# Rests and waits of a hand-written schedule: a two-layer trunk, GLA and sparse attention, on one core

## The chip, the cores and the metric

One core of a Trainium2 chip runs the whole computation as one program. TensorE (PE) does the matrix products, VectorE (DVE) and ScalarE (ACT) the elementwise work, GpSimd (POOL) a little, and SyncE (SP) issues nearly all DMA transfers. The metric is the device time of one execution in microseconds (us), as the median of several.

## What is computed

The reference, cut to the two layers that run (x is 1024 tokens by 1024 features, float32):

```python
def reference(x, p, positions, ...):
    for i in range(DEPTH):                       # DEPTH = 2: gla_mixer, then dsa_mixer
        y = mixer_i(x)
        x = layer_norm(ALPHA * x + y, ln_g[i], ln_b[i])
        x = x + (p[i] @ ple_w[i]) * sigmoid(x @ ple_gate_w[i])
    return x

def gla_mixer(x, ...):       # 4 heads, chunks of 64, dk 256, dv 512
    q, k, v, z, a = split(x @ w_in)
    g = log_sigmoid(a @ w_a2 + b_a) / 16; G = cumsum(g) in the chunk
    o = tril((q e^G)(k e^-G)^T) v + (q e^G) S    # S = e^G_last S + (k e^(G_last-G))^T v
    return (norm(o) * gn_g * silu(z)) @ w_out

def dsa_mixer(x, ...):       # 16 heads of 128, one k and one v for all of them
    q, k, v, z, qi, ki, wi = split(x @ w_in); rope on q, k, qi, ki
    score = sum over 8 index heads of relu(qi ki^T) * wi, causal
    keep the 256 keys of highest score for each query
    return (softmax(q k^T, on the kept keys) v * silu(z)) @ w_out
```

## The kernel before

Every product is made of three: operands are split into a high part and a remainder (`split`, L419 on ACT makes the high part, L411 on DVE subtracts), and high x high, low x high and high x low are summed. Weights are split on the way in as well: `wst` is loaded, ACT makes `whi` (L189) and DVE `wlo` (L191, L193).

The tokens go through in two halves of 512 (HT). Layer 0 (GLA) runs half 0 and half 1, four heads each (GH = 4). Inside a head, chunk pairs c = 0 to 3 pass four steps, s1 to s4; s3 makes the output `ot` from PE's `o` (the DVE copy L785), s4 transposes it on PE (`oT`), multiplies by z (L849) and splits the product into `u` (L411), which the output projection reads as `pb<-whi,u`. For some c the way goes by DRAM in squares (`od`, L801, L807) and ends in L826 and L823 instead; in the last head c = 3 goes by `oT` in both halves, c = 2 only in half 0. Then come the layer norm, the gate (L1002, L1000, L1001), and the new x, stored as `x2s` (L1464) and split for layer 1. Layer 1 (sparse attention) has, for each half, slots -1 to 15, one for each head: products of q, scores S with the selection as an added bias, softmax, transposes of the weights through DRAM (`sqd`, `PT`), split of those (`ph` on ACT, L1679; `PT` on DVE, L1677), the product with v (`o`), and the output projection with its sum in y (L878). A slot of half 0 is some 11 to 22 us long.

What sets the order is a planner that runs while the program is written. `Flow` keeps a planned PE time, `fl.now`, which each matmul advances; steps are put into a heap with due times (`fl.at`, `after`, `chain`) and are written into the program when the planned time has reached theirs. `fl.ripe(t)` holds a step back to planned time t, in tries 0.3 apart; `fl.need(have)` runs due steps until something is there. Engines then take their instructions strictly as written, so the plan decides who stands behind whom, and semaphores decide when each may go.

Two kinds of work are spread thinly over others by a `Background`, one step each `gap` of planned time, none before `due`:

```python
def pace(self, now):
    if self.gen is not None and now >= self.due:
        self.due = max(self.due, now - 2.0) + self.gap
        self.step()
```

`bg3` splits layer 1's weights ahead during layer 0 (`split_ahead`, gap 2.06): for each of 130 cuts of 128x512, a load into `pst` (L223), the high part `phi` on ACT (L233), its store `whs` (L235), the remainder on DVE (L237), its store `wls` (L239). What is left of it at the end of layer 0 is written out at once (`bg3.finish()`, L1517). `bg` runs the rope tables first and, in half 0 of layer 1, the selection (`topk_steps`): for each of the bits of a threshold one count on DVE (L1197, tile 640 wide) and three on ACT (L1241, tiles 768 to 1024 wide) with a few small DVE rows (L1247, L1248, L1250); for the last bit the three tiles are read again from DRAM (`sc<-sc_s`, L1234) and all four are counted on DVE, then L1202 and the rows after it make the bias of each tile (to L1270). `bg.finish()` (L1940) writes out what is left when half 0 ends.

`load_p` (L899) loads two tiles of the token embeddings p for the gate and splits them after a wait; `q_phase` (L1551) puts q of a head through its rope (L1052 to L1057) and splits it a wait of 3.0 later.

Of the kernel before, what the change touches and what calls it, by code (L numbers as in the profile page):

```python
# [23 lines left out]
HT = 512  # L24
NK = 8
GH = 4
# [251 lines left out]
def trunk_kernel(ctx, tc, x_tok, x_T, p_T, pos, freq, g_q, g_k, g_v, g_z, g_a, g_a2, g_ba, g_gn, g_o,  # L278
# [134 lines left out]
    def split(hi, lo, src, done=None):  # L413

        def second():
            lo_part(lo, src, hi)
            if done:
                done()
        chain((0, lambda: act.activation(hi, src, AF.Copy)), (0.9, second))  # L419
# [253 lines left out]
    def core_steps(u):  # L673
# [92 lines left out]
        def s3(c):  # L766
            def f():
                cs = slice(c * 128, c * 128 + 128)
                fl.req(("A", c) in st, v[c] is not None, not has_state(c) or ("S", c) in st)
                fl.ripe(st["At", c] + 2.2)  # L770
                Ah, Al = st.pop(("A", c))
                vh, vl = v[c]
                ps = pp.tile([128, 512], F32, tag="o", name="o")
                ops = [(Ah, vh), (Al, vh), (Ah, vl)]
                if has_state(c):
                    for d, (sh, sl) in enumerate(st.pop(("S", c))):
                        ops += [(qh[:, d, cs], sh), (ql[:, d, cs], sh), (qh[:, d, cs], sl)]
                for i, (l, r) in enumerate(ops):
                    mm(ps, l, r, i == 0, i == len(ops) - 1)
                ot = lp.tile([128, 512], F32, tag="ot", name="ot", bufs=2)  # L780
                if by_square(c):
                    dve.transpose(ot.rearrange("p (m b i) -> p b m i", m=4, b=4), ps)  # L782
                    after(2.2, lambda: squares_out(c, ot))
                else:
                    dve.tensor_copy(ot, ps)  # L785
                junk = lp.tile([128, 512], BF16, tag="junk", name="junk")
                act.activation(junk, ps, AF.Square, accum_out=u["ss"][:, c:c + 1])  # L787
                st["o", c] = ot
                st["ot", c] = fl.now
                u["late"] = c == 3  # L790
                if c < 3:
                    after(0.3, lambda: make_S(c + 1))
            return f
# [41 lines left out]
        def s4(c):  # L835
            def f():
                if by_square(c):
                    return
                cs = slice(c * 128, c * 128 + 128)
                fl.req(("o", c) in st, "z" in u, h == 0 or u["prev"].get("out", 0) > c)  # L840
                fl.ripe(st["ot", c] + (2.6 if h == GH - 1 else 1.1))
                ot = st.pop(("o", c))
                ps = pp.tile([128, 4, 128], F32, tag="oT", name="oT")
                for b in range(4):
                    fl.transpose(ps[:, b], ot[:, b * 128:b * 128 + 128], ident)
                uf = lp.tile([128, 4, 128], F32, tag="uf", name="uf", bufs=2)
                uh, ul = t2k("u", F32R), t2k("u", F32R)

                chain((0, lambda: dve.tensor_mul(uf, ps, u["z"][:, :, cs])),  # L849
                      (0.8, lambda: split(uh, ul, uf.rearrange("p b t -> p (b t)"), lambda: made(c, uh, ul))))  # L850
            return f
# [43 lines left out]
    def load_p(layer, half, alloc, wait, stage):  # L895
        P = []
        for k in range(2):
            st = stage(k)
            nc.sync.dma_start(st, p_T[layer, k, :, half * HT:half * HT + HT])  # L899
            ph, pl = alloc(), alloc()  # L900
            after(wait, lambda ph=ph, pl=pl, st=st: split(ph, pl, st))
            P.append((ph, pl))
        return P
# [142 lines left out]
    def rope(x, c, s, swap, tmp, then, wait=1.2):  # L1046
        ab = []

        def first():
            ab[:] = tmp()[:x.shape[0]], tmp()[:x.shape[0]]  # L1050
            a, b = ab
            dve.tensor_mul(b, x, c)  # L1052
            dve.stream_shuffle(a, x, swap)  # L1053
            dve.tensor_mul(a, a, s)

        def second():
            dve.tensor_add(x, *ab)  # L1057
        chain((0, lambda: None), (0.8, first), (1.6, second), (wait, then))
# [484 lines left out]
    def q_phase(st, h, X):  # L1543
        def ev(ps):
            qf = small_tile("qf")
            fl.need(lambda: h < 2 or st.get(("A", h - 2)) == 3)
            qh, ql = small_tile("q", F32R, 4), small_tile("q", F32R, 4)

            def done():
                st["q", h] = qh, ql  # L1550
            act.activation(qf, ps, AF.Copy)  # L1551
            rope(qf[0:32], tabs[0], tabs[1], swap_h, tmp2, lambda: split(qh, ql, qf, done), 3.0)

        yield from fm_block(("dq", h), X, ev)

# [294 lines left out]
    for half in range(NH):  # L1850
# [12 lines left out]
        S = [attend(st, h, half, ap, sq) for h in range(16)]  # L1863
        for h, units in enumerate(plan, -1):
            start = st["slot"] = fl.now
            bg.gap = 1.4 if h == 15 else 1.75 if h > 3 and h % 4 < 2 else 1.5
            if h == 15:
                fl.at(start + 5.0, lambda: setattr(bg, "due", max(bg.due, fl.now + 24.0)))
            dur = sum(len(u[1]) if u[0] == "o" else 1 for u in units) * B + core * (1.0 if h >= 0 else 0.5)
            if h >= 0:  # L1870
                _, parts, pvs, _, loads, scale = S[h]
                lead = 9.0 if half else 7.4
                step = (dur - lead - 2.4) / len(parts)
                if half:
                    fl.at(start + 1.5, loads[1])
                    early, first, gap = 3, 6.6, 1.2
                else:
                    early, first, gap = 3, max(5.0, 21.5 - last_dur), 1.3
                fl.at(start + (5.0 if half else 3.5), scale[1])
                for i in range(early):  # L1880
                    fl.at(start + first + gap * i, parts[i])
                spread(parts[early:], start + lead + early * step, dur - lead - 2.4 - early * step)
                if h == 15 and half:
                    spread(pvs, start + 10.2, 4.2)
                else:
                    spread(pvs, start + lead + 2.9, dur - lead - 2.4)
            if h < 15:
                first, _, _, stores, loads, scale = S[h + 1]
                spread(first, start + 0.3, 5.8 if half else 4.4)
                for i, f in enumerate(stores):  # L1890
                    fl.at(start + (10.0 if half else 7.0) + 0.5 * i, f)
                fl.at(start + (dur - 3.0 if h == 14 or h < (1 if half else 5) else 12.0 if half else 8.5), scale[0])
                if half:
                    fl.at(start + (max(dur - 1.0, 18.0) if h >= 0 else 16.0), loads[0])
                else:
                    fl.at(start + 13.0, loads[0])
            last_dur = dur
            if h == 14:
                Pt = load_p(1, half, lambda: small_tile("q", F32R, 4), dur + 2.5,
                            lambda k: xp.tile([128, HT], F32, tag="xst", name="xst", bufs=2))  # L1900
            if h == -1:
                if half:
                    yt = new_y()
                y5 = yt.rearrange("p k (a t i) -> p (k a) t i", a=4, t=4)

                def y(t, a, n, y5=y5):
                    return y5[:, a // 32:(a + n) // 32, t]
                normed = {}

                def to_rows(t, y=y, normed=normed):  # L1910
                    normed[t] = [xp.tile([128, HT], F32, tag="x", name="yn", bufs=16) for _ in range(2)]
                    return [(r.rearrange("p (x i) -> p x i", i=32), y(t, 512 * i, 512)) for i, r in enumerate(normed[t])]

                def rows(t, a, n, normed=normed):
                    return normed[t][a // 512][:, a % 512:a % 512 + n]
                for k in range(NK):
                    fl.at(start + (4.0 if half else 14.0) + 3.0 * k, lambda k=k: back(st, yt, k, kept[half, k]))
            if half == 0 and 4 <= h < 12:
                rows_ahead(1, h - 4, lambda n: xp.tile([128, HT], F32, tag="xst", name="xk", bufs=2), start + 2.0)
            fl.run(*(unit(u) for u in units))  # L1920
        norm, y_done = norm_steps(y, l1, EPS / ALPHA ** 2, to_rows, (0, 1))
        if half == 0:
            X = XT()
            feed_by(feed_x2(X, 1), fl.now + 21.0, 2.3)
        for u in last_outs:
            fl.run(unit(u, norm if u[1:2] == ((7,),) else None))
        fl.drain()
# [77 lines left out]
```

## Time and profile before

| | us |
|---|---|
| median of 3 runs | 1933.72 (1933.07 to 1934.30) |
| profiled execution | 1935.66 |
| its span in the trace | 1933.8 |
| PE busy | 1914.8 (99%) |
| DVE busy | 1497.3 (77%) |
| ACT busy | 1000.7 (52%) |
| end of layer 0 in the trace | about 1000.6 |
| half 0 of layer 1, slots 0 to 15 | 1096.6 to 1452.1 |
| half 1 of layer 1 begins | about 1452 |

Times below are measured from the span's start. A row of the timeline reads: start, duration, engine, line, operation, tile written <- tiles read, size, and in square brackets how long the engine stood idle before it and whose result ended that. A row of the waits reads: the engine and the tile that waited, the engine and tile waited for, the total, the number of times, the longest. SP's rows are the issuing of DMAs, not their transfer. Where a row's x stands over 1, several instructions are drawn together. PE's next matmul overlaps the end of the one before, so successive starts 0.227 apart are full speed for the products of 512 columns.

### The profile page before, as it was taken

The numbers are of one execution on the slowest core, as the hardware profiler recorded it, in microseconds if no ns is written. First come the engines' busy times: TensorE is split into PE (matmuls) and PEld (weight loads), VectorE is DVE, ScalarE is ACT, GpSimd is POOL, SyncE is SP. The second block draws the span as 40 slices with busy tenths as digits, with TensorE's granted clock in tenths as the row PEclk, the third lists the DMA queues.
The fourth block names the chain that finished last, engine by engine and source line by source line (L and its number), as shares of the span: only waits on it lengthen the run. The fifth ranks groups of instructions, "written<-read, shape, count | busy, mean of one in ns | idle before, by whom it ended". The sixth has DMA issues, their size and how long they took to land.

```text
span 1933.8 us, 26931 instructions
## 1 busy us (share of the span) xinstructions
PE 1914.8 (99%) x8806; PEld 1588.1 (82%) x8806; DVE 1497.3 (77%) x3089; ACT 1000.7 (52%) x1896; POOL 171.6 (9%) x337
## 2 busy tenths in 40 slices
PE   9999999999999999999999999999999999999999
PEld 7888888888888888888888788888888778888877
DVE  5777666796778888888859987778798887777873
ACT  5564636445564646464635576666443444434432
POOL 0101010110010101010101001221001010000000
PEclk9999999999999999999999999999999999999999
DMA  4667776768667767776687598887878998888873
GB/s 156 227 210 251 226 238 217 234 207 279 226 212 264 242 229 251 221 244 220 208 300 283 184 305 288 302 307 272 312 234 296 307 311 300 301 304 291 292 273 140
DMA packets 202108, 491.53 MB, mean 254 GB/s; under 512 B 27080, under 2 KB 43504, under 8 KB 195824
## 3 DMA queue, kind: packets, MB, share of 16 engines
q1 hardware_dynamic: 193200, 474.55, 72.2%
q0 software_dynamic: 8768, 15.27, 2.4%
q8 instruction: 69, 1.13, 0.2%
q14 instruction: 71, 0.58, 0.1%
HBM read 344.49 MB, written 145.23 MB: 253 GB/s over the span
## 4 chain that ended last, share of the span: by engine, by line
PE 82%; DVE 9%; DMA 4%; ACT 3%; issue 2%; SPq 0%; DVEq 0%; ACTq 0%
PE pb L58 62%; PE o L58 7%; PE U L58 6%; PE S L58 5%; DMA PT<-sqd 2%; PE tr L58 1%; DVE sc L1175 1%; DVE tk L1197 1%; DVE PT L1677 1%; DMA inv<-row 1%; DVE sq L1639 0%; DVE tk L1264 0%; DMA wst<-in_g_v 0%; PE xt L62 0%; DVE rt L1053 0%
## 5 line engine op out<-in xcount | busy, mean ns | idle before, releaser
L58 PE MATMUL pb<-x,whi 128*128 128x512 f32 x2272 | 704.1, 391 | 0.8 <-DVE x L411 0.7
L58 PEld LDWEIGHTS pb<-x,whi 128*128 128x128 f32 x2272 | 419.5, 188 | 80.1 <-DVE x L411 1.9
L58 PE MATMUL pb<-x,wlo 128*128 128x512 f32 x1136 | 442.6, 390 | 0.0
L58 PE MATMUL pb<-whi,u 128*128 128x512 f32 x1024 | 339.9, 392 | 3.3 <-DVE u L411 1.3
L58 PEld LDWEIGHTS pb<-x,wlo 128*128 128x128 f32 x1136 | 213.2, 188 | 45.5 <-DVE wlo L191 0.4
L58 PEld LDWEIGHTS pb<-whi,u 128*128 128x128 f32 x1024 | 192.1, 188 | 44.1 <-DVE u L411 2.2
L58 PE MATMUL pb<-wlo,u 128*128 128x512 f32 x512 | 199.6, 390 | 0.0
L191 DVE TENSOR_TENSOR wlo<-wst,whi 128x512 fp32r<-128x512 f32 x232 | 154.2, 684 | 33.3 <-ACT whi L189 31.7
L189 ACT ACTIVATE whi<-wst 128x512 fp32r<-128x512 f32 x232 | 136.0, 622 | 80.7 <-DMA wst<-in_g_k 26.9
L1633 ACT ACTIVATE sq<-P,mx 128x128 f32<-128x128 f32 (+7 forms) x128 | 98.7, 772 | 88.1 <-DVE mx L1626 62.4
L58 PE MATMUL S<-kT,q 128*128 128x512 f32 (+2 forms) x576 | 123.7, 343 | 2.0 <-DVE q L411 1.2
L1679 ACT ACTIVATE ph<-PT 128x512 fp32r<-128x512 f32 (+2 forms) x160 | 86.0, 558 | 64.8 <-PE o L58 40.0
L58 PEld LDWEIGHTS S<-kT,q 128*128 128x128 f32 x576 | 100.3, 188 | 21.1 <-DVE mx L1626 2.1
L58 PEld LDWEIGHTS pb<-wlo,u 128*128 128x128 f32 x512 | 96.2, 188 | 18.2
L1677 DVE TENSOR_TENSOR PT<-PT,ph 128x512 fp32r<-128x512 f32 (+2 forms) x160 | 92.6, 592 | 22.8 <-ACT ph L1679 22.5
L1241 ACT ACTIVATE tk<-sc,tki 128x768 f16<-128x768 f32 (+2 forms) x90 | 92.9, 1033 | 25.4 <-DVE tki L1250 21.6
L1639 DVE STREAM_TRANSPOSE sq<-sq 128x128 f32<-128x128 f32 (+7 forms) x128 | 97.7, 768 | 1.3 <-ACT sq L1633 1.2
L787 ACT ACTIVATE junk<-o 128x512 bf16<-128x512 f32 x32 | 19.1, 597 | 146.0 <-DVE ot L782 125.2
L58 PE MATMUL o<-ph,vT 128*128 128x512 f32 (+2 forms) x320 | 91.2, 366 | 0.5 <-ACT ph L1679 0.3
L237 DVE TENSOR_TENSOR pst<-pst,phi 128x512 fp32r<-128x512 f32 x130 | 88.6, 682 | 1.6 <-ACT phi L233 1.6
L58 PE MATMUL pb<-whi,x 128*128 128x512 f32 x256 | 85.8, 392 | 0.3 <-DVE x L411 0.3
L58 PE MATMUL U<-whi,x 128*128 128x512 f32 x256 | 84.8, 390 | 0.0
(338 smaller groups left out, 3416.9 us busy)
## 6 DMA issues: line engine op xcount, KB each, us to landing
whi<-whs SPq DMA_DIRECT2D x128, 512.0 KB, 6.2
wlo<-wls SPq DMA_DIRECT2D x128, 512.0 KB, 7.3
sqd<-sq SPq DMA_DIRECT2D x192, 256.0 KB, 4.8
PT<-sqd SPq DMA_DIRECT2D x48, 1024.0 KB, 7.5
whs<-phi SPq DMA_DIRECT2D x130, 256.0 KB, 4.3
wls<-pst SPq DMA_DIRECT2D x130, 256.0 KB, 4.2
wst<-in_g_z SPq DMA_DIRECT2D x32, 512.0 KB, 4.5
wst<-in_g_o SPq DMA_DIRECT2D x32, 512.0 KB, 4.3
```

Source lines behind the costliest of these rows:

```text
L58: self.pe.matmul(out, lhsT, rhs, start=start, stop=stop)
L189: self.nc.scalar.activation(hi[:, c], st[:, c], AF.Copy, scale=1.0 if gain is None else gain)
L191: self.nc.vector.tensor_sub(lo[:, c], st[:, c], hi[:, c].bitcast(F32))
L237: self.nc.vector.tensor_sub(st, st.bitcast(F32), hi.bitcast(F32))
L787: act.activation(junk, ps, AF.Square, accum_out=u["ss"][:, c:c + 1])
L1175: dve.scalar_tensor_tensor(d, r[:, :e], w, d, op0=OP.mult, op1=OP.add)
L1197: dve.tensor_scalar(junk()[:, :n], scs[j], thr_ap, None, op0=op, op1=OP.add, accum_out=cnt[:, j:j + 1])
L1241: act.activation(junk()[:, :n], scs[j], AF.Sign, bias=cand[:, j:j + 1].bitcast(F32), accum_out=cnt[:, j:j + 1])
L1633: act.activation(to, rows, AF.Exp, scale=-1.0, bias=mx, accum_out=sm[:, t:t + 1])
L1639: dve.transpose(x, x)
L1677: dve.tensor_sub(lo, lo.bitcast(F32), hi.bitcast(F32))
L1679: chain((0, lambda: act.activation(hi, lo.bitcast(F32), AF.Copy)), (0.8, second))
```

## The change

Five places of the planner's numbers change. (1) When `ot` of c = 3 of the last head is made, `bg3` rests for 7 us of planned time, in both halves. (2) `s4` of c = 3 waits 1.9 instead of 2.6 after `ot`, and in half 0 that of c = 2 waits 1.1. (3) The third head's q is split 1.8 after its rope's start, the others' still 3.0. (4) The selection's gap is 1.45 instead of 1.5 where it was 1.5, and in half 0 it rests for 10 us from the start of the slot h = 4. (5) In slot 14 the loads of the embeddings are put 6 us after the slot's start; the splits stay at their planned time.

```diff
                 u["late"] = c == 3
+                if c == 3 and h == GH - 1:
+                    bg3.due = max(bg3.due, fl.now + 7.0)
...
-                fl.ripe(st["ot", c] + (2.6 if h == GH - 1 else 1.1))
+                fl.ripe(st["ot", c] + (1.9 if c == 3 else 1.1))
...
-            rope(qf[0:32], tabs[0], tabs[1], swap_h, tmp2, lambda: split(qh, ql, qf, done), 3.0)
+            rope(qf[0:32], tabs[0], tabs[1], swap_h, tmp2, lambda: split(qh, ql, qf, done), 1.8 if h == 2 else 3.0)
...
-            bg.gap = 1.4 if h == 15 else 1.75 if h > 3 and h % 4 < 2 else 1.5
+            bg.gap = 1.4 if h == 15 else 1.75 if h > 3 and h % 4 < 2 else 1.45
+            if h == 4 and not half:
+                bg.due = max(bg.due, start + 10.0)
...
             if h == 14:
-                Pt = load_p(1, half, lambda: small_tile("q", F32R, 4), dur + 2.5,
-                            lambda k: xp.tile([128, HT], F32, tag="xst", name="xst", bufs=2))
+                def get_p(half=half, wait=dur + 2.5 - 6.0):
+                    Pt[:] = load_p(1, half, lambda: small_tile("q", F32R, 4), wait,
+                                   lambda k: xp.tile([128, HT], F32, tag="xst", name="xst", bufs=2))
+                Pt = []
+                fl.at(start + 6.0, get_p)
...
+        fl.need(lambda: Pt)
         for u in last_outs:
```

Because the plan decides the order, these numbers move rows on several engines, some far from the edit. In the rows below the line numbers of the kernel after are two above those of before from L791 on (L1464 is L1466 there, and so on; below that line they are the same), up to L1865; from there they lie further apart.

SP at the end of layer 0, from the last x split's store to the loads for layer 1, before (`kI` reads index keys kept in DRAM, `ix` the index rope's sine and cosine):

```order
L1464 DMA x2s<-x_9542 128x512
L1464 DMA x2s<-x_9552 128x512
L235 DMA whs<-phi 128x512
L239 DMA wls<-pst 128x512
L1788 DMA kI<-kv_s 128x512 x2
L1065 DMA ix<-rope_s 128x512
```

and now, the last store of x being the first row:

```order
L1466 DMA x2s<-x_9532 128x512
L235 DMA whs<-phi 128x512
L223 DMA pst<-in_gate_c 128x512
L239 DMA wls<-pst 128x512
L235 DMA whs<-phi 128x512
L239 DMA wls<-pst 128x512
L235 DMA whs<-phi 128x512
L239 DMA wls<-pst 128x512
L1790 DMA kI<-kv_s 128x512 x2
L1067 DMA ix<-rope_s 128x512
```

One load, two whs and two wls more stand between the last store of x and `kI`.

DVE in slot 4 of half 0, where PE waits for the first `PT`, before:

```order
L1054 TENSOR_TENSOR rt<-rt,tab_9954 32x512
L1197 TENSOR_SCALAR tk,tkf<-sc_9958,tki 128x640
L878 TENSOR_TENSOR y<-pb,y 128x16x32
L1677 TENSOR_TENSOR PT<-PT,ph 128x4x128
L1057 TENSOR_TENSOR qf<-rt 32x512
```

and now:

```order
L1056 TENSOR_TENSOR rt<-rt,tab_9954 32x512
L880 TENSOR_TENSOR y<-pb,y 128x16x32
L1679 TENSOR_TENSOR PT<-PT,ph 128x4x128
L1059 TENSOR_TENSOR qf<-rt 32x512
L1679 TENSOR_TENSOR PT<-PT,ph 128x4x96
```

The count has left its place; the sum into y still stands ahead of PT.

SP near the end of half 0, where the score tiles are read again for the last bit (`xst<-x2s` are the x of half 1, `whi` and `wlo` weights split ahead), before:

```order
L1572 DMA xst<-x2s 128x512
L1234 DMA sc_9960<-sc_s 128x896
L1234 DMA sc_9961<-sc_s 128x1024
L174 DMA whi<-whs 128x1024
L174 DMA wlo<-wls 128x1024
L174 DMA whi<-whs 128x1024
L174 DMA wlo<-wls 128x1024
L1572 DMA xst<-x2s 128x512 x2
```

and now:

```order
L1574 DMA xst<-x2s 128x512
L1236 DMA sc_9959<-sc_s 128x768
L174 DMA whi<-whs 128x1024
L174 DMA wlo<-wls 128x1024
L1236 DMA sc_9960<-sc_s 128x896
L174 DMA whi<-whs 128x1024
L174 DMA wlo<-wls 128x1024
L1574 DMA xst<-x2s 128x512
L1236 DMA sc_9961<-sc_s 128x1024
L1574 DMA xst<-x2s 128x512
```

The widest tile's read has moved behind both weight pairs and one load of x.

## The prediction

> **What bounds the kernel now.** I read the page's totals first, then what TensorE (PE) waits for over the whole run, then the timeline around each of those waits.
>
> ```profile
> span 1933.8 us, 26931 instructions
> PE 1914.8 (99%) x8806; PEld 1588.1 (82%) x8806; DVE 1497.3 (77%) x3089; ACT 1000.7 (52%) x1896; POOL 171.6 (9%) x337
> PEclk9999999999999999999999999999999999999999
> PE o L58 <- DVE PT L1677: 4.7, 7, 1.6
> PE pb L58 <- DVE u L411: 1.3, 1, 1.3
> PE S L58 <- DVE q L411: 1.2, 1, 1.2
> PE pb L58 <- DVE x L411: 0.9, 3, 0.4
> PE pb L58 <- DVE z L1562: 0.5, 1, 0.5
> PE pb L58 <- DVE u L823: 0.5, 1, 0.5
> ```
>
> PE is busy 99% of the span at the full clock, and the change alters no matmul. So the time can only move by PE's waits: 1933.8 less 1914.8 leaves 19.0 us, and no gain can exceed that. The rows give total, times and longest; nearly every wait is for one DVE instruction, because DVE and ACT run their instructions in the written order and something else stood ahead of the needed one. The question for each part is therefore what stands ahead of the needed instruction now, and what stands ahead of another one instead.
>
> **The change part by part.** All sums are made against the profiled execution (1935.66 us, span 1933.8); the runs' median is 1933.72, and I add the sum to that median.
>
> *Pause of the splitting ahead, last GLA head, half 0.*
>
> ```profile
> 400.70 0.68 DVE L785 COPY ot<-o 128x512 f32<-128x512 f32 x1
> 402.29 0.60 PE L62 MATMUL oT<-ident,ot 128*128 128x128 f32 x4
> 408.76 0.68 DVE L411 TENSOR_TENSOR u<-uf,u 128x512 fp32r<-128x512 f32 x1
> 409.50 0.73 PE L58 MATMUL pb<-whi,u 128*128 128x512 f32 x2 [1.33 <-DVE u L411]
> ```
>
> The order now puts this L411 five DVE rows sooner (two of the splitting's L237 and three more, some 0.6 to 0.7 each), so the 1.33 goes. The shorter rest of c == 3 puts the oT transposes six matmuls sooner; six at the 0.227 between starts are 1.36, so 400.93, but the copy they read ends at 401.38. PE then waits about 0.5 there. Term: -0.83 (from -1.33, if the copy is sooner too, to -0.5).
>
> *The same in half 1.*
>
> ```profile
> 925.41 0.50 PE L58 MATMUL pb<-whi,u 128*128 128x512 f32 x1 [0.28 <-ACT u L820]
> 925.88 0.68 DVE L823 TENSOR_TENSOR u<-uf,u 128x512 fp32r<-128x512 f32 x1
> 926.61 0.73 PE L58 MATMUL pb<-whi,u 128*128 128x512 f32 x2 [0.46 <-DVE u L823]
> ```
>
> PE loses 0.28 + 0.46 = 0.74 now. In the new order c == 3's product L849 and its L411 stand ahead of the last L823, which PE needs first; counting DVE's rows on from the transposes, L823 ends near 926.95 and PE waits 1.1. Term: +0.4 (from -0.74, if all goes, to +0.9).
>
> *What the two pauses leave for the end of layer 0.* Each pause is 7 us at one step per 2.06, so about 7 steps are put off, and the rest is issued at once when the layer ends: after the last x split now come three phi on ACT, three L237 on DVE and whs, wls, whs, wls, whs, wls on SP, where one of each came before.
>
> ```profile
> 997.46 5.76 SPq L1464 DMA_DIRECT2D x2s<-x  x2
> 1003.31 0.38 SPq L235 DMA_DIRECT2D whs<-phi  x1
> 1004.89 0.32 SPq L239 DMA_DIRECT2D wls<-pst  x1
> 1006.52 0.32 SPq L1065 DMA_DIRECT2D ix<-rope_s  x1
> 1011.54 0.68 DVE L1052 TENSOR_TENSOR rt<-z,ix 64x512 f32<-64x512 f32 x1 [6.68 <-DMA ix<-rope_s]
> 1050.68 0.50 PE L58 MATMUL pb<-x,whi 128*128 128x512 f32 x1 [0.33 <-DVE x L411]
> DMA  9999999721000019999910199934989999797755
> wls<-pst SPq DMA_DIRECT2D x5, 256.0 KB, 2.0
> pst<-in_gate_c SPq DMA_DIRECT2D x3, 256.0 KB, 3.9
> ```
>
> (The DMA row is 1000 to 1010 in slices of 0.25; the two last rows are medians from issue to landing in 975 to 1012.) The third phi needs the last pst load, issued about 1004.5, right behind the first whs. Its landing lies between the 2.0 and the 3.9 of those rows; the queues have idle slices here, so I take 3.0: phi from 1007.5, 0.6 for it and 0.6 for the subtraction, wls near 1008.8 instead of 1004.89. Everything behind on SP is 3.9 late: the kI loads, the two ix loads of the rope table and the weights after them. DVE has already waited 6.68 for ix, and from 1011.54 it runs with hardly a pause to the x splits for which PE waits at 1050.68 (0.9 in the three x rows of the waits). So nearly all arrives at PE: 3.9 less 0.45 that one idle stretch of DVE takes up. Term: +3.5 (0, if there is more slack than I see, to +5).
>
> *Third head's q.* Its wait of 1.2 at the head's scores stands behind another head's rope on DVE; q's own split is now issued ahead of that rope on ACT and DVE. Term: -1.19 (all or nothing; half 1 shows no such wait).
>
> *The selection's rest in half 0's fifth slot.*
>
> ```profile
> 1170.31 0.86 DVE L1197 TENSOR_SCALAR_CACHE_REDUCE tk<-sc,tki 128x640 f16<-128x640 f32 x1
> 1171.11 0.67 DVE L878 TENSOR_TENSOR y<-pb,y 128x512 f32<-128x512 f32 x1
> 1171.71 0.67 DVE L1677 TENSOR_TENSOR PT<-PT,ph 128x512 fp32r<-128x512 f32 x1
> 1172.43 0.50 PE L58 MATMUL o<-PT,vT 128*128 128x512 f32 x1 [1.60 <-DVE PT L1677]
> ```
>
> The count L1197 (0.80 to the next start) leaves the place, and three ACT counts leave the ACT queue ahead of ph, so ph and PT start sooner by more than the wait. Term: -1.6 (-0.7 if only the DVE count counts).
>
> *Embeddings loaded 6 us later in slot 14.* In SP's order the inv row load now stands ahead of the two embedding loads and a count no longer stands ahead of z.
>
> ```profile
> 1369.91 0.69 DVE L1740 TENSOR_TENSOR z<-z,inv 128x512 f32<-128x512 f32 x1 [3.11 <-DMA inv<-row]
> 1372.39 0.68 DVE L1562 SCALAR_TENSOR_TENSOR z<-z,pb 128x512 f32<-128x512 f32 x1
> ```
>
> PE's 0.5 for this z goes. The embeddings' splits stand where they stood, and their data then has 6 us less, which the 5 us of a load in this stretch (below) just covers. Term: -0.49 (0 to -0.5).
>
> *What the rest does to the end of the selection.* Resting 10 us and going 0.05 faster per step ends it two steps later. So at the end of half 0 the last reload of a score tile (sc from sc_s, 512 KB) now stands on SP behind a pair of weight loads that waits for its buffer until 1416.74, where it went out at 1406 before, and its last bit's count and the threshold rows behind it stand later on DVE.
>
> ```profile
> 1417.15 0.38 SPq L174 DMA_DIRECT2D wlo<-wls  x1
> 1418.37 1.27 DVE L1197 TENSOR_SCALAR_CACHE_REDUCE tk<-sc,tki 128x1024 f16<-128x1024 f32 x1
> 1423.68 0.69 DVE L411 TENSOR_TENSOR x<-xst,x 128x512 fp32r<-128x512 f32 x1 [0.50 <-ACT x L419]
> 1462.55 0.67 DVE L1052 TENSOR_TENSOR rt<-qf,tab 32x512 f32<-32x512 f32 x1
> 1466.11 2.22 PE L58 MATMUL S<-kT,q 128*128 128x384 f32 x9 [0.21 <-ACT q L419]
> sc<-sc_s SPq DMA_DIRECT2D x1, 512.0 KB, 6.1
> whi<-whs SPq DMA_DIRECT2D x6, 512.0 KB, 5.1
> ```
>
> From 1423.68 DVE runs without a pause to the rope L1052 of half 1's first q, for which PE already waits at 1466. Whatever is put behind 1423.68 is paid. Issued at 1418.05, the reload lands at 1423.2 by 5.1 or 1424.1 by 6.1; the count of 1.21 then starts there instead of at 1418.37, and the next x split starts at 1424.4 to 1425.3 instead of 1423.68 (+0.7 to +1.6); 2.15 of threshold rows that were done before 1423 come on top. Term: +3.5 (+2.15 if the data is there in time, 4.1 above, and 0 if DVE has slack that I don't see).
>
> [...]
>
> *Other moves* of selection steps and splitting steps by a place or two: +0.3 (-0.7 to +1.3), from waits of 0.1 to 0.8 that half 1's first slots show now.
>
> Sum: -0.83 + 0.4 + 3.5 - 1.19 - 1.6 - 0.49 + 3.5 + 0.3 = +3.6, so 1937.3 on the median (the profiled execution would read near 1939.3).
>
> **The rivals.** (a) *Both new delays are hidden*, since the order shows places and not times: without the two +3.5 the sum is -3.4, 1930.3; if the second head part costs nothing either, -4.6, 1929.1, which is faster. It speaks for it that five of the waits are single, named and moved away from; against it, the two places where PE already waits for the delayed DVE chain (0.33 and 0.21 above). (b) *One of the two is hidden*: +0.1, 1933.8. (c) *Heavier*: the layer-end burst carries its 5, the reload 4.1, others +1.3, and the fifth slot doesn't do what it says, since L878 still stands ahead of L1677 there and only the count's 0.86 is won: 3.6 + 1.5 + 0.6 + 1.0 + 0.74 = +7.4, 1941.1. It decides from a pst landing over 4 us on.
>
> **How the numbers follow.** A measurement of this kernel tells about 0.2%, 3.9 us, from no change: 1929.85 to 1937.59. My forecast 0.46 (own range 1935.5 to 1939.2, of which 0.26 lies below 1937.59); one delay hidden 0.20; both hidden 0.14, of which 0.10 under 1929.85; heavier 0.20. Faster 0.10, same 0.26 + 0.20 + 0.04 = 0.50, slower 0.20 + 0.20 = 0.40. The range leaves a tenth at each end: 1931.0 to 1940.8.
>
> **What would show it.** Right: no PE wait for u L411 near 408, for S near 1113 or for PT near 1170; wls at 1008 to 1010 on SP ahead of ix, L1052 at 1015 and x waits of over 3 us in all before slot -1; a DVE idle of some 4 us for sc before the last L1197 near 1420, and a wait of over 3 for q at the start of half 1. Wrong: SP reaching ix by 1007, or that wait staying under 1. A PE wait over 1 us at a place not named here would also break the sum.

## The result, and the profile after

The kernel after takes 1944.17 us (median of 6, 1942.28 to 1945.72) against 1934.01 before (median of 6): the ratio is 1.0052, 95% interval 1.0041 to 1.0064. It is slower by 10 us, outside the range of 1931.0 to 1940.8. Totals and the longest rows of PE's waits, from the profile after:

```profile
span 1943.2 us, 26906 instructions
PE 1917.9 (99%) x8806; PEld 1590.4 (82%) x8806; DVE 1498.1 (77%) x3089; ACT 1001.0 (52%) x1896; POOL 171.7 (9%) x337
PE S L58 <- ACT q L419: 4.4, 1, 4.4
PE o L58 <- DVE PT L1679: 4.4, 7, 1.3
PE pb L58 <- DVE u L825: 2.1, 1, 2.1
PE pb L58 <- DVE x L411: 1.4, 3, 0.9
PE o L58 <- ACT ph L1681: 1.1, 1, 1.1
PE oT L62 <- DVE ot L785: 0.5, 1, 0.5
```

Two things stand in these rows. The waits for u L411 (1.3) and S for DVE q L411 (1.2) are gone as the change meant, and new waits of 4.4 and 2.1 have come. And PE is *busy* 3.1 us longer with the same 8806 matmuls. That can't be a wait; the matmuls themselves became slower. The next two views show where. The first is the table by stretches around the wait of 4.4 (start and end, length, busy time and number of instructions of PE, its weight loads, DVE, ACT and POOL, then the granted clock, the third number from the right, the DMA share and GB/s); the second is PE's timeline behind the wait of 2.1:

```profile
1465.00:1475.00 10.00, 5.64 (x25) 4.32 (x24) 9.68 (x12) 1.23 (x2) 3.29 (x1) 0.98 0.36 120
1475.00:1480.00 5.00, 4.97 (x19) 4.23 (x20) 2.94 (x9) 2.23 (x4) 4.00 (x8) 0.69 1.02 417
1480.00:1500.00 20.00, 20.00 (x95) 16.70 (x94) 13.26 (x29) 5.67 (x12) 0.54 (x1) 1.00 0.90 291
```

```profile
927.69 0.73 PE L58 MATMUL pb<-whi,u 128*128 128x512 f32 x2 [2.13 <-DVE u L825]
928.26 0.40 PE L58 MATMUL pb<-wlo,u 128*128 128x512 f32 x1
928.49 1.01 PE L58 MATMUL pb<-whi,u 128*128 128x512 f32 x2
929.31 0.63 PE L58 MATMUL pb<-wlo,u 128*128 128x512 f32 x1
929.73 1.05 PE L58 MATMUL pb<-whi,u 128*128 128x512 f32 x2
930.59 0.63 PE L58 MATMUL pb<-wlo,u 128*128 128x512 f32 x1
931.01 1.05 PE L58 MATMUL pb<-whi,u 128*128 128x512 f32 x2
```

From 928.49 on three matmuls take 1.24 to 1.28 (929.73 less 928.49, 931.01 less 929.73), where at a granted clock of 1.00 they take 0.68 (924.04 to 924.72 in the same trace; three times 0.227); the granted clock is 0.69 in the five us from 1475 on, behind the other wait, and 1.00 again after. So each of these two waits was paid twice: once as a wait, and then by slower products, start to start some 0.42 instead of 0.227 for each of 512 columns. By the slip defined next this cost 1.6 us behind the wait of 2.1 and 1.1 us behind that of 4.4.

To see where the rest went I compare the start of the n-th matmul after with that before (both have 8806, in nearly the same order) and take what this difference (the slip) gains in each stretch. The single-part experiments below are set beside it; each is one profiled execution.

| place | predicted | after | with one part alone |
|---|---|---|---|
| last GLA head, half 0 | -0.83 | -0.9 | -0.9 (pauses) |
| last GLA head, half 1 | +0.4 | +2.7 | +0.3 (pauses) |
| end of layer 0 to slot -1 | +3.5 | +3.1 | +4.6 (pauses) |
| third head's q, and the 40 us behind it | -1.19 | -1.4, then +0.7 | -1.4, then +0.3 (q) |
| fifth slot, half 0 | -1.6 | -1.9 | -1.9 (rest) |
| slots 14 and 15, half 0 | -0.49 | +0.8 | -0.8 (embeddings), +0.7 (rest) |
| layer norm behind half 0 | 0 | +0.9 | +0.9 (rest) |
| end of half 0 to half 1's first q | +3.5 | +5.2 | +6.2 (rest), -0.5 to -0.6 (others) |
| last slots of half 1 | 0 | +1.3 | +1.2 (embeddings) |
| sum of all stretches | +3.6, with +0.3 for other moves | +9.3 | |

The sum also holds stretches that are not listed: +0.9 in layer 0 outside the last heads, and -1.9 in half 1's middle slots. No part made the latter: in each of the ten traces set against that of before (after and the first nine experiments) this stretch is 1.4 to 2.9 shorter, and in the last three 0.0 to 1.3. That the profiled execution of before was itself long there fits its 1935.66 against a median of 1933.72; it is not shown otherwise.

The two places that answer to the prediction's main terms, SP and DVE after:

```profile
1007.32 0.33 SPq L223 DMA_DIRECT2D pst<-in_gate_c  x1
1012.01 0.69 SPq L239 DMA_DIRECT2D wls<-pst  x1
1013.72 0.42 SPq L1067 DMA_DIRECT2D ix<-rope_s  x1
1017.87 0.68 DVE L1054 TENSOR_TENSOR rt<-z,ix 64x512 f32<-64x512 f32 x1 [5.88 <-DMA ix<-rope_s]
1421.90 0.38 SPq L174 DMA_DIRECT2D wlo<-wls  x1
1422.81 0.42 SPq L1236 DMA_DIRECT2D sc<-sc_s  x1
1429.27 1.28 DVE L1199 TENSOR_SCALAR_CACHE_REDUCE tk<-sc,tki 128x1024 f16<-128x1024 f32 x1 [4.43 <-DMA sc<-sc_s]
```

The last wls leaves 7.12 later than before (1012.01 less 1004.89), 2.66 of which PE was late already there: 4.5 for the burst, where 3.9 was forecast. The last score tile is read behind the weight pair and one load of x, lands 6.4 after its issue, and DVE stands idle for 4.43 as forecast.

### The profile page after: what moved, and what is told of

It reads as the page before. It is cut to its first block, busy times and chain, and to the rows that moved or that the text cites. A ratio compares the mean times of both kernels' runs of the same rounds, so it can differ in the third digit from the quotient of the medians.

```text
span 1943.2 us, 26906 instructions
## 1 busy us (share of the span) xinstructions
PE 1917.9 (99%) x8806; PEld 1590.4 (82%) x8806; DVE 1498.1 (77%) x3089; ACT 1001.0 (52%) x1896; POOL 171.7 (9%) x337
## 4 chain that ended last, share of the span: by engine, by line
PE 82%; DVE 7%; DMA 6%; ACT 2%; issue 1%; SPq 1%; DVEq 0%; ACTq 0%
PE pb L58 62%; PE o L58 7%; PE U L58 6%; PE S L58 5%; DMA PT<-sqd 2%; PE tr L58 1%; DVE sc L1177 1%; DVE sq L1641 1%; DMA wls<-pst 1%; DMA wlo<-wls 1%; DVE PT L1679 1%; DVE tk L1199 0%; DMA wst<-in_g_v 0%; DMA vT<-kv_s 0%; ACT rt L1181 0%
## 5 line engine op out<-in xcount | busy, mean ns | idle before, releaser
L233 ACT ACTIVATE phi<-pst 128x512 fp32r<-128x512 f32 x130 | 80.5, 620 | 9.3 <-DMA pst<-in_gate_c 3.4
```

Source lines behind the costliest of these rows:

```text
L233: self.nc.scalar.activation(hi, st.bitcast(F32), AF.Copy)
```

## The experiments

**One part alone, four kernels.** The code of after, with one of its edits each; before ran at 1934.01 (29 runs) on the same chip.

```diff
 e1_pause: before, plus
+                if c == 3 and h == GH - 1:
+                    bg3.due = max(bg3.due, fl.now + 7.0)
...
+                fl.ripe(st["ot", c] + (1.9 if c == 3 else 1.1))
 e2_rest: before, plus
+            bg.gap = 1.4 if h == 15 else 1.75 if h > 3 and h % 4 < 2 else 1.45
+            if h == 4 and not half:
+                bg.due = max(bg.due, start + 10.0)
 e3_q: before, plus
+            rope(..., lambda: split(qh, ql, qf, done), 1.8 if h == 2 else 3.0)
 e4_emb: before, plus
+                def get_p(half=half, wait=dur + 2.5 - 6.0):
...
+                fl.at(start + 6.0, get_p)
```

> The kernel before with only the two pauses of the splitting ahead and the shorter rests of s4. Theory, from the slip of TensorE in the trace after (start of the n-th matmul, after less before): -0.9 at the last GLA head of half 0, +3.0 at that of half 1 (1.4 more of waiting and 1.6 of a slower clock behind a wait of over 2 us), +3.2 at the end of layer 0: +5.3, so about 1939. Rival: the losses come only with the other parts (a collision), and these two alone give -0.8 to +1, 1933 to 1935.

Measured: 1938.79, ratio 1.0024 (1.0015 to 1.0034), +4.8. The end of layer 0 costs +4.6 by itself, part of it a new wait for the weights that now come late. At the last GLA head of half 1 PE waits only 1.4 and stays fast (the mean granted clock of this execution is 1.000), +0.3:

```profile
PE pb L58 <- DVE x L411: 1.7, 3, 0.9
PE pb L58 <- DVE u L825: 1.4, 1, 1.4
PE pb L58 <- DMA whi<-whs: 1.0, 1, 1.0
```

The theory's +5.3 is about the measured sum, but not its +3.0 at that head: the code of this head is the same in both kernels, so what differs is the execution. The timeline of DVE shows it. In the trace after, one product waits for the tile that comes back from DRAM; in this kernel's it starts without a wait (first row after, second row this kernel):

```profile
923.04 0.69 DVE L828 TENSOR_TENSOR uf<-uf,z 128x512 f32<-128x512 f32 x1 [0.66 <-DMA uf<-od]
```

```profile
922.77 0.68 DVE L828 TENSOR_TENSOR uf<-uf,z 128x512 f32<-128x512 f32 x1
```

Two of the kernels below (e5 and e6) have this code of layer 0 as well. Over the four traces DVE's idle for that tile is 0, 0, 0.36 and 0.66, and PE's wait 1.39, 1.39, 1.83 and 2.13; only the last is followed by slow products. So of the +2.7 here some part is the luck of one execution.

> The kernel before with only the selection's rest in the fifth slot and the gap of 1.45. Theory: the wait for PT in that slot goes (-1.9 with its start-to-start share), the last reload of a score tile is late and half 1's first q makes TensorE wait 4 us and then run slowly for 3 us (+5.2): +3.3, about 1937, with a wait S<-q of about 4 near 1465. Rival: the selection ends late only because the layer's end is late too: -1.6 to -1.9, about 1932, and that wait stays under 1.

Measured: 1938.38, ratio 1.0025 (1.0014 to 1.0035), +4.4. The theory holds: the fifth slot gains 1.9 and the wait for q comes without any lateness from layer 0. The rival is out.

```profile
PE S L58 <- ACT q L419: 4.6, 1, 4.6
PE o L58 <- DVE PT L1677: 2.4, 4, 0.9
```

Not foreseen: +0.7 in slot 15 and +0.9 at the layer norm behind it. At the layer norm ACT's last two counts now stand:

```profile
1405.23 1.14 ACT L1241 ACTIVATE tk<-sc,tki 128x1024 f16<-128x1024 f32 x1
1408.50 0.66 PE L62 MATMUL S<-ident,yn 128*128 128x128 f32 x4 [0.66 <-ACT x L978]
```

Before, this count ran at 1375.58. Two steps later in the plan became 30 us later on the chip. The kernel already lets the selection rest for 24 us of planned time from 5 us into slot 15 (`bg.due = max(bg.due, fl.now + 24.0)`), and the two steps no longer come ahead of that rest. What costs the 0.7 in slot 15 is not shown.

> The kernel before with only the third head's q split sooner. Theory: the wait of 1.2 near 1113 goes and nothing else comes: -1.2 to -1.5, about 1932.4. Rival: a slower stretch of TensorE some 15 us behind it, which the trace after shows and the one before does not, belongs to this part and gives half of it back: -0.8.

Measured: 1931.98, ratio 0.9988 (0.9979 to 0.9997), -2.0. The trace has -1.4 at the head and +0.3 behind it. The sign is sure; the sizes of theory and rival (-1.2 to -1.5, or -0.8) are closer than the interval tells apart.

> The kernel before with only the embeddings loaded 6 us later in slot 14. Theory: the wait for z in slot 15 goes (-0.5 to -0.8), but the later loads stand ahead of the stores and loads of the last head's softmax weights, so PT comes late in slot 15 of both halves (+1.6 in half 0, +1.1 in half 1): +1.5 to +2, about 1935.5. Rival: that lateness belongs to the selection's counts in slot 14 and 15 (half 0) and this part alone gives -0.5, 1933.4.

Measured: 1934.28, ratio 1.0004 (0.9994 to 1.0013), no change to be seen. Each hypothesis had half of it right. In half 0 the part alone gains 0.8 and PT isn't late, so that lateness comes with the selection's part (+0.7 there with the rest alone), as the rival said. In half 1 the two loads of the embeddings leave SP 4.6 us ahead of the last head's stores of softmax weights, where before they stood between the loads of the head ahead of it; the last head's first load of PT then leaves 0.9 later against PE's matmuls than before, and PE waits. By which transfer the lateness comes is not shown:

```profile
1851.31 0.73 PE L58 MATMUL o<-ph,vT 128*128 128x512 f32 x2 [1.05 <-ACT ph L1679]
```

The four differences add up to +7.4, where the whole change measured +10.2. Going by the profiled executions, 1.6 of what is missing is the slow stretch at the last GLA head of half 1, which the trace after has and that of the pauses alone has not.

**The suspected causes taken away from the kernel after, and the gains kept.** Before ran at 1933.76 (21 runs).

```diff
 e5_gap142: after, with
-            bg.gap = ... else 1.45
+            bg.gap = ... else 1.42
 e6_reload_queue: after, with
-                    nc.sync.dma_start(scs[j], sc_s[i, :, :scs[j].shape[1]])
+                    nc.gpsimd.dma_start(scs[j], sc_s[i, :, :scs[j].shape[1]])
 e7_no_burst: after, with
-                    bg3.set(W.split_ahead(later, lp, xp), 2.06)
+                    bg3.set(W.split_ahead(later, lp, xp), 2.01)
 e8_kept_gains: before, with
+  if c == 3 and h == GH - 1 and not half: bg3.due = max(bg3.due, fl.now + 7.0)
+  fl.ripe(st["ot", c] + ((2.6 if u["half"] else 1.9) if c == 3 else 1.1))
+  bg3.set(W.split_ahead(later, lp, xp), 2.03)
+  1.8 if h == 2 else 3.0;  gap 1.42 with the rest;  embeddings late in half 0
```

> The kernel after with the selection's gap 1.42 instead of 1.45, so that the rest is made up and the last reload of a score tile stands ahead of the weight pair on SP again. Theory: the wait of 4.4 for half 1's first q and the slow 3 us behind it go: 5 to 6 us under the kernel after, about 1938.5. Rival: DVE has too much work at the end of half 0 in any order (the rest and the late layer end push it there), the wait stays over 2 us and the time near 1943.

Measured: 1937.01, ratio 1.0015 (1.0006 to 1.0024), 7 us below the kernel after. The wait for q is gone (-0.6 in that stretch, as in the kernels without the rest), and with it the 0.9 at the layer norm. So the wait and the late counts came from 0.03 per step. In slot 15 this kernel still loses 1.0 behind its gain, so the rest is not wholly free. The rival is out. Of the 7 us, going by the traces, 1.6 is the slow stretch at the last GLA head of half 1, which this execution has not.

> The kernel after with the three reloads of score tiles issued by GpSimd instead of SP, so that the last one does not stand behind the weight pair that waits for its buffer; all else in its place. Theory: two causes share the wait for half 1's first q, the late reload (1.4 to 2.4) and the threshold rows that now come late (2.15): the wait falls from 4.4 to 2 to 3 and the time by 2, to about 1942. Rival A, the reload is all: wait under 0.7, 1938. Rival B, the reload is nothing: wait still over 4, 1944.

Measured: 1939.96, ratio 1.0025 (1.0012 to 1.0039), 4 below the kernel after. Both causes are there, as the theory says, and both rivals are out; but the read is the larger part. With it early, DVE no longer stands idle for the tile, and PE's wait falls by 2.8, to 1.6 instead of the 2 to 3 expected. What is left is 1.4 more than the 0.21 of before, where the late rows had been put at 2.15.

```profile
PE S L58 <- ACT q L419: 1.6, 1, 1.6
```

Behind this wait PE ran slowly too (1.5 us lost; the mean granted clock is 0.999), though it is under 2.

> The kernel after with the splitting's gap 2.01 instead of 2.06, so that no step is left at the end of layer 0 and SP issues the kI loads right behind the last store of x. Theory: the 3 to 4.5 us that TensorE loses between the end of layer 0 and slot -1 go: about 1940.5. Rival: that loss is the lateness of the whole layer and stays, or the closer steps cost as much inside the GLA heads: 1943 to 1945.

Measured: 1944.82, ratio 1.0055 (1.0038 to 1.0072), as slow as the kernel after. The place is shown and the remedy fails, as the rival said: from the end of layer 0 to slot -1 the loss is 0.0, the kI loads leave right behind x2s and the x waits are those of before, but with the closer steps the stretches of layer 0 outside the last heads lose 2.5 (0.9 in the kernel after), and PE slows behind two waits again (the mean granted clock is 0.997), 2.5 in the last head of half 1 and 4.9 for half 1's first q:

```profile
1008.39 0.32 SPq L1466 DMA_DIRECT2D x2s<-x  x1
1008.83 0.86 SPq L1790 DMA_DIRECT2D kI<-kv_s  x2
```

```profile
PE pb L58 <- DVE u L825: 2.5, 1, 2.5
PE pb L58 <- DVE x L411: 0.9, 3, 0.4
```

> The kernel before with what gained only: third head's q sooner, the selection's rest with gap 1.42, the pause and the shorter rests in GLA's half 0 alone with the splitting's gap 2.03 (one cut left at the layer's end as before), embeddings late in half 0 alone. Theory: -0.9 (last GLA head of half 0) - 1.4 (q) - 1.5 to -1.9 (fifth slot) - 0.5 (slot 15) = -4.3 to -4.7, about 1929.5, with no slow stretch of TensorE. Rival: places that nothing here names (the first slots of half 1, the layer's end) give back 2 or more: 1932 to 1934.

Measured: 1932.08, ratio 0.9987 (0.9978 to 0.9997), no better than the third head's q alone, and what the rival said. The gains of layer 1 are in the trace (-1.4, -1.9); layer 0 gives +2.4 back with its closer steps, at waits such as 1.7 for the copy ot in the very head that the pause was for:

```profile
PE oT L62 <- DVE ot L785: 1.7, 1, 1.7
```

**The best of it, and a ladder of waits.** Before ran at 1933.41 (23 runs). The ladder lays multiplications by 1.0 ahead of three splits for which PE waits anyway; the values don't change.

```diff
 e9_q_rest: before, with
+  1.8 if h == 2 else 3.0;  gap 1.42 with the rest;  embeddings late in half 0
 e10, e11, e12: before, with
+    hold = lambda n, t: [dve.tensor_scalar(t, t, 1.0, None, op0=OP.mult) for _ in range(n)]
+  n ahead of split: last GLA head's u (half 0)  1, 3, 0
+                    third head's q (half 0)     2, 1, 4
+                    half 1's first q            4, 2, 6
```

> The kernel before with the third head's q sooner, the selection's rest with gap 1.42, and the embeddings late in half 0 alone; nothing of GLA changed. Theory: -1.4 (q), -1.5 to -1.9 (fifth slot), -0.5 (slot 15): -3.5, about 1930.3, two below the version that also had the pause in GLA's half 0 with a closer splitting. Rival: the gains of layer 1 do not add up (the first slots of half 1 take them back), about 1932.

Measured: 1930.09, ratio 0.9982 (0.9973 to 0.9991), -3.3 for a forecast of -3.5. It is faster than both kernels. The waits for PT fall from 4.7 to 2.7, those for q and z are gone, and layer 0 is as before:

```profile
span 1927.5 us, 26925 instructions
PE o L58 <- DVE PT L1677: 2.7, 5, 0.8
PE pb L58 <- DVE u L411: 1.3, 1, 1.3
```

> The kernel before with multiplications by 1.0 on DVE (values unchanged) ahead of three splits for which TensorE already waits: one ahead of u of the last GLA head of half 0 (wait of 1.33 before), two ahead of the third head's q (1.19), four ahead of half 1's first q (0.2). Theory: what slows TensorE is the length of the wait, and above about 2 us it runs near half speed for some 3.4 us behind it: waits of 1.7 or less leave the spacing of 0.227 at once, waits over 2 are followed by 0.41 to 0.43. Rival: it depends on the run (where the wait falls), so equal waits sometimes slow it and sometimes not.

Measured: 1940.18 (ratio 1.004, 1.0025 to 1.0055). The waits became 1.77, 1.98 and 2.16, and a slow stretch follows all three (mean granted clock 0.997); the theory had left 1.7 to 2 open.

> As the ladder before it, with three, one and two multiplications at the three places. Theory: a slow stretch behind each wait over 2 us and behind none under 1.7. Rival: no fixed length decides.

Measured: 1937.48 (ratio 1.0019, 1.0009 to 1.0029). Waits 1.85, 1.53 and 1.10, and no slow stretch behind any (mean granted clock 1.000).

> As the ladders before it, with none, four and six multiplications at the three places. Theory: the wait at u stays 1.3 without a slow stretch; the two others are over 2.5 and each is followed by a slow stretch of the same length, about 3.4 us, however long the wait: each costs its wait and some 1.6 us. Rival: a longer wait is followed by a longer slow stretch.

Measured: 1941.55 (ratio 1.0041, 1.0026 to 1.0056). Waits 1.33, 1.98 and 3.26; slow behind the two longer ones, with the clock low for 3.41 us each time, at a cost of 1.6 and 1.25. Two multiplications more moved the second wait no further than in the first ladder, 1.98 in both.

The same place in two of them, a wait of 1.77 and one of 1.85:

```profile
410.53 0.73 PE L58 MATMUL pb<-whi,u 128*128 128x512 f32 x2 [1.77 <-DVE u L413]
...
412.18 1.05 PE L58 MATMUL pb<-whi,u 128*128 128x512 f32 x2
413.03 0.63 PE L58 MATMUL pb<-wlo,u 128*128 128x512 f32 x1
```

```profile
411.20 0.73 PE L58 MATMUL pb<-whi,u 128*128 128x512 f32 x2 [1.85 <-DVE u L413]
...
412.70 0.61 PE L58 MATMUL pb<-whi,u 128*128 128x512 f32 x2
413.15 0.39 PE L58 MATMUL pb<-wlo,u 128*128 128x512 f32 x1
```

So neither hypothesis is whole. Over all fourteen traces, leaving out the first microseconds, in which products still start 0.50 to 0.73 apart (in the trace after until 7.05): all nine waits of 1.98 to 4.87 are followed by a slow stretch; of the twelve from 1.57 to 1.85 two are (1.57 and 1.77) and ten are not; no shorter one is.

The length of a wait alone does not sort these: 1.57 and 1.77 are among the slow ones, 1.83 and 1.85 are not. In each of these traces the times at which the granted clock changes, 50 in all, lie on one grid with steps of 3.413 us, to within 0.01 us (after: 928.53, 931.94, 1474.66 and 1478.07, of which the first and the third lie 160 steps of 3.4133 apart). Between a run's start and its end the clock was low for one step or for two, in no case for another length. What went with a low step is how long PE stood idle, summed, in the step ahead of it: ten steps with 1.98 us or more were all followed by a low one; 1.67, 1.70 and 1.77 were followed by one, 1.80 and 1.81 were not; 1.61 and less never was. Here are grid steps of the kernel after (the wait of 2.13), of the rest alone (4.60), and of the first and the second ladder (1.77 and 1.85); the first busy time is PE's:

```profile
925.12:928.53 3.41, 1.28 (x6) 0.72 (x6) 3.38 (x6) 2.10 (x4) 0.00 (x0) 1.00 0.37 76
928.53:931.94 3.41, 3.41 (x10) 2.63 (x9) 2.00 (x4) 0.00 (x0) 0.00 (x0) 0.50 0.69 217
```

```profile
1465.35:1468.76 3.41, 0.96 (x5) 0.46 (x3) 3.34 (x7) 0.00 (x0) 1.16 (x1) 1.00 0.45 124
1468.76:1472.18 3.42, 1.27 (x4) 1.04 (x5) 2.63 (x4) 0.63 (x1) 3.42 (x3) 0.50 0.96 355
1472.18:1475.59 3.41, 3.41 (x13) 2.93 (x12) 2.22 (x8) 1.93 (x2) 2.71 (x6) 0.50 1.02 416
```

```profile
408.40:411.81 3.41, 1.64 (x8) 1.06 (x7) 3.37 (x6) 1.11 (x4) 0.00 (x0) 1.00 0.88 294
411.81:415.23 3.42, 3.42 (x10) 2.64 (x9) 2.88 (x5) 1.20 (x3) 0.00 (x0) 0.50 0.86 247
```

```profile
409.41:412.82 3.41, 1.62 (x7) 1.35 (x8) 3.38 (x6) 1.10 (x3) 0.00 (x0) 1.00 0.47 181
412.82:416.23 3.41, 3.41 (x17) 2.83 (x16) 3.38 (x6) 1.29 (x3) 0.00 (x0) 1.00 0.89 300
```

The wait of 4.60 covers 2.45 of one step and 2.15 of the next, and two low steps follow; that of 4.87 covers 3.17 and 1.70, and two follow as well; those of 4.39 and 3.26 have one low step. So the two longest waits here have a slow stretch of 6.83 us instead of 3.41, as the rival to the last ladder said. By the slip the eleven slow stretches cost 1.1 to 2.0 us, 1.6 in the middle. What decides between 1.67 and 1.81 is not shown.

## Why the prediction was wrong, point by point

*Two steps failed.* The first is the opening of the argument, that PE is at the full clock and the time can only move by waits. It took the clock of before for a constant, which it was not: the change made two waits of over 2 us, behind each of them the granted clock was 0.50 for 3.41 us, and the slow products there cost 1.6 and 1.1 more. A wait of 3.5 was even forecast at half 1's first q, so the price was on the table and its second half was not. The second is three places put at a gain or at nothing: slots 14 and 15 (-0.49, measured +0.8), the layer norm (0, measured +0.9) and the last slots of half 1 (0, measured +1.3), 3.5 together. The sum was +3.6 and the medians differ by 10.2.

*The signs.* The three old waits are gone, DVE stands idle for the score tile and PE waits 4.4 for q, all as forecast. The x waits before slot -1 are not: they come to 1.4 in all, where over 3 was forecast, and the +3.1 is spread over several waits (0.8 for z L1143 and 0.4 for weights among them). Two waits over 1 stand at places that were not named, 1.3 for PT in slot 15 of half 0 and 1.1 for ph in half 1; that was the sign that the sum is broken.

*End of the selection*, +3.5: the order on SP and the idle of DVE are right, and the kernel with the read on another queue shows that both the read and the late rows count. Their sizes are not right: 2.8 for the read, where 0.7 to 1.6 was put, and 1.4 for the rest, where 2.15 was put. Measured +5.2 there, against -0.6 without it: 4.2 of new wait and the rest the slow clock. The term also left out what the late counts do on ACT at the layer norm, +0.9; I had followed only the last counts on DVE. The read took 6.4, where 5.1 to 6.1 was put.

*Last GLA head, half 1*, +0.4: +0.3 when the tile from DRAM is there in time, +2.7 in the trace after, where it wasn't: 1.6 of that is the slow clock. The order puts L828 ahead of the split that PE needs, and I counted rows without asking what they wait for. The +0.3 comes from a wait of 1.4, where 1.1 was forecast, so that it is so near +0.4 is partly luck.

*End of layer 0*, +3.5: +3.1 and +4.6; it falls to 0.0 without the burst. The mechanism is right and the bounds held, though the x waits show only part of it.

*Last GLA head of half 0, third head's q, fifth slot*: -0.83, -1.19 and -1.6 against -0.9, -1.4 and -1.9. The rows give PE's gap; from start to start each wait is some 0.2 longer (before, 407.78 to 409.50 is 1.72 where 0.227 is usual, for a gap of 1.33), so all three came out larger. The forecast's new wait of 0.5 for the copy ot is in the rows above. Behind the third head +0.3 to +1.0 came back, which I hadn't seen, and whose cause is not shown.

*Embeddings*, -0.49: -0.8 in half 0 by itself, a little more than forecast. Half 1 I took for 0 from the order alone; it cost 1.2.

The heavier rival was the nearest, and still 3 us short. Its reload of 4.1 came (4.2 of new wait), and so did more than its 1.3 for others; the burst did not reach its 5 in the kernel after, and the fifth slot did what the forecast says. The slow clock was none of its terms.

Open: what decides between 1.67 and 1.81 us of idle in a grid step, and why the four parts add to 2.8 less than the whole; 1.6 of it is the slow stretch that only some executions have.

## What to carry to other kernels

Look twice at the price of a long TensorE wait. In the fourteen traces here all nine waits of 1.98 us or more, and two of the twelve from 1.57 to 1.85, were followed by slow products that cost another 1.1 to 2.0 us, and no shorter wait was; so two waits of 1.2, well apart, would cost less here than one of 2.5 that merges their delays, as an estimate from these numbers. When background work is made to rest, find where its remaining steps end up and give it the pace to be done in time: here 1.42 instead of 1.45 was worth 7 us by the medians (1937.01 against 1944.17), while a denser pace in the tight layer gave back all it saved (1944.82). When counting the rows that stand ahead of the needed one on an engine, look for what each of them waits on, DMAs first: in the trace after DVE stood idle 0.66 for a tile from DRAM in one such row and 4.43 in another.

## What was not expected of the hardware

Waits of only 2 us on TensorE were followed by a lower clock, all nine from 1.98 us on. In every trace here the granted clock changed only on a grid of 3.413 us and went to 0.50 for whole steps: 3.41 us in nine cases of the fourteen traces and 6.83 in two, at 0.41 to 0.43 from start to start for a matmul of 512 columns, against 0.227. Behind waits of 1.57 to 2.51 this began 0.3 to 1.3 us after PE had resumed, at the next point of the grid (0.84 behind the wait of 2.13 in the trace after, 927.69 to 928.53); behind 3.26 and more PE resumed at the low clock, or within 0.1 us of it: such a point lay in the wait or just behind it (1474.66 for the wait of 4.39, which ended at 1475.03). The mean granted clock of a whole run shows it in the third digit: 0.997 to 0.999 in the six runs of the kernel after, 1.000 in all eleven runs of the best version. One step of 3.41 us at 0.50 takes 0.0009 off a mean over 1943 us, so the six runs had, as an estimate, one to three such steps; the one with 0.999 is the fastest of them, 1942.28.
